# A hybrid recurrent trunk layer: the down projection's residual rows, affine steps, gated sums and buffers are rearranged

## The chip, the cores and the metric

The program runs on one core of a Trainium2 chip. The metric is the device time of one execution in microseconds. Engines are called as the profile calls them: PE (TensorE), DVE (VectorE), ACT (ScalarE), POOL (GpSimd) and SP, whose queue issues nearly all DMAs. Each engine works through its own queue in order.

## The reference, cut to what matters

2048 latent tokens and 128 context tokens pass one layer: a mixer with an input and an output projection, a norm, a SwiGLU feed-forward network (FFN) and a second norm. What the change touches is the part from the first norm on:

```python
    y, s_f, s_b = hybrid_mixer(h, ...)
    x = layer_norm(DEEPNORM_ALPHA * x + gate1 * y, ln1_g, ln1_b)
    h = x * (1.0 + scale2) + shift2
    ffn = (jax.nn.silu(h @ w_ffn_gate) * (h @ w_ffn_up)) @ w_ffn_down
    x = layer_norm(DEEPNORM_ALPHA * x + gate2 * ffn, ln2_g, ln2_b)
```

The model width is 1024, the FFN width 2816. All tensors are float32.

## The kernel before

**Arithmetic.** Tokens are handled in 17 rows of 128 tokens (16 of latents, one of context, number NS = 16). Each float32 factor of a matmul is split into a rounded high half (a copy on ACT, L129) and the low remainder (a subtraction, on DVE at L135, or on POOL at L133 if asked). `mm3` (L138 to L140) then issues three matmuls, high by high, high by low and low by high.

**Out projection** (lines from L1220 on). For each row it loads y and x (`xr`), multiplies out of PSUM by the gate (L1241), adds `ALPHA * x` (L1247), takes the norm's statistics (L893, L895; 1/std in two short POOL steps, L886 and L887), and normalises with one tensor_scalar (L1249). The normalised row, without the norm's gain and bias, is stored to `x1_d` (L1250); it is also transposed for the FFN, whose matrices take gain and bias in another place. `xr` has two buffers, in turns.

**Down projection** (from L1325). One level of a seven-product scheme (as in Strassen-Winograd) computes the product of activations and down weights: both are halved along the FFN width, the weights along the output columns, the tokens in pairs of rows. The combined activations lie in `dA[0..6]`, the combined weights in `td`. The stage has two halves `g` of eight rows each; a half has seven products `o`, a product eleven k-tiles, in six steps `kk` of two (the last of one), with four PSUM tiles (cells `q`). So one product has 11 x 4 x 3 = 132 matmuls of 512 columns. The leftover row (context) adds 33 matmuls to products 0, 2, 3 and 4 of the second half (`lk`), and to product 3 also a second weight (`wx`).

Every step loads raw weights (`ws`, three buffers, or `x0..`/`x2..`, kept from the first half for products 0 and 2) and raw activations (`as`, two buffers), and splits both (`wh`/`wl`, `ah`/`al`, three buffers each). After a product its four PSUM tiles are copied or added into cell tiles `c0`, `c1` (PSUM has seven buffers for them). A residual row is loaded from `x1_d`, and POOL multiplies it by the first norm's gain and adds its bias, both scaled by ALPHA (L1410, L1411). `fold` multiplies a finished sum by the gate (L1425), adds it to the row (L1426) and takes statistics (L1427). `finish` normalises the row on DVE (L1439) and applies the second norm's gain and bias on POOL (L1442, L1443), then stores it. The deferred steps stand in a list `bg`, from which one is taken after each step `kk` (BG = 1).

In the very last product the cells are computed one after the other from its third step on (KZ = 2), with split weights and activations in extra buffers; `last_fin` then ends the four last rows, two with ACT and POOL steps, two on DVE (L1450 to L1473).

**What sets the order.** A planner orders each engine's queue from the program order, from priorities (the first two steps of the stage are raised by DP = 400) and from a model of durations. Pools are stacked in SBUF; a tile at an address that a tile of an earlier stage held waits for that tile's last use.

## Time and profile before

| | us |
|---|---|
| median of 3 runs (2572.86 to 2576.82) | 2573.5 |
| profiled execution | 2574.1 |
| its span, first to last instruction | 2572.1 |

| engine | busy us | share of the span |
|---|---|---|
| PE | 2430.5 | 94% |
| DVE | 1953.7 | 76% |
| ACT | 1045.2 | 41% |
| POOL | 292.5 | 11% |

The profile is of one execution. A busy share is an average over stages; a stage is read from a window. In the lists a line such as `wl<-ws,wh` means an instruction that writes tile `wl` and reads `ws` and `wh`. A line number can be that of a helper (L129, L133, L135, L138 to L140), so tiles tell more than lines. "Idle before" is the time in which the engine stood still before an instruction, with what ended it.

### The profile page before, as it was taken

The numbers are of one execution on the slowest core, as the hardware profiler recorded it, in microseconds if no ns is written. First come the engines' busy times: TensorE is split into PE (matmuls) and PEld (weight loads), VectorE is DVE, ScalarE is ACT, GpSimd is POOL, SyncE is SP. The second block draws the span as 40 slices with busy tenths as digits, with TensorE's granted clock in tenths as the row PEclk, the third lists the DMA queues.
The fourth block names the chain that finished last, engine by engine and source line by source line (L and its number), as shares of the span: only waits on it lengthen the run. The fifth ranks groups of instructions, "written<-read, shape, count | busy, mean of one in ns | idle before, by whom it ended". The sixth has DMA issues, their size and how long they took to land. (4 is left out here: it accounts for less than half of the span.)

```text
span 2572.1 us, 38336 instructions
## 1 busy us (share of the span) xinstructions
PE 2430.5 (94%) x14628; PEld 2195.1 (85%) x14628; DVE 1953.7 (76%) x2995; ACT 1045.2 (41%) x1660; POOL 292.5 (11%) x227
## 2 busy tenths in 40 slices
PE   8999999999998998999999999999999889888995
PEld 6888888998887787899999999999999768666774
DVE  7755666887767655588887888878998676897768
ACT  4434445646457332433333333344444333233431
POOL 0000000000000113000000000000000251654035
PEclk9999999999999999999999999999999899899997
DMA  8954543434545377656434655336543745535552
GB/s 319 304 173 136 160 157 101 153 117 149 159 131 166 117 235 232 217 188 198 149 110 141 191 203 188 127 124 219 208 170 112 268 158 190 199 128 161 186 175 106
DMA packets 264295, 445.32 MB, mean 173 GB/s; under 512 B 32048, under 2 KB 174640, under 8 KB 264112
## 3 DMA queue, kind: packets, MB, share of 16 engines
q1 hardware_dynamic: 245488, 374.47, 44.8%
q10 hardware_dynamic: 18624, 68.42, 7.7%
q8 instruction: 114, 1.87, 0.3%
q14 instruction: 69, 0.57, 0.1%
HBM read 311.86 MB, written 130.94 MB: 172 GB/s over the span
## 5 line engine op out<-in xcount | busy, mean ns | idle before, releaser
L1018 PE MATMUL g<-xh,gwl 128*128 128x384 f32 (+1 forms) x1848 | 607.1, 329 | 8.5 <-DVE gwl L135 8.5
L1016 PE MATMUL g<-xh,gwh 128*128 128x384 f32 (+1 forms) x1848 | 608.5, 329 | 0.1
L1017 PE MATMUL g<-xl,gwh 128*128 128x384 f32 (+1 forms) x1848 | 606.5, 328 | 1.5 <-DVE xl L135 1.5
L1018 PEld LDWEIGHTS g<-xh,gwl 128*128 128x128 f32 x1848 | 348.1, 188 | 10.6 <-DVE gwl L135 10.5
L1017 PEld LDWEIGHTS g<-xl,gwh 128*128 128x128 f32 x1848 | 348.3, 188 | 2.9 <-DVE xl L135 1.8
L1016 PEld LDWEIGHTS g<-xh,gwh 128*128 128x128 f32 x1848 | 348.1, 188 | 1.7 <-issue 1.0
L139 PE MATMUL da<-wl,ah 128*128 128x512 f32 x588 | 241.3, 410 | 32.3 <-DVE wl L135 32.2
L138 PE MATMUL da<-wh,ah 128*128 128x512 f32 x588 | 239.5, 409 | 13.3 <-ACT wh L129 7.2
L140 PE MATMUL da<-wh,al 128*128 128x512 f32 x588 | 239.9, 408 | 6.3 <-DVE al L135 6.3
L129 ACT ACTIVATE ah<-as 128x1024 fp32r<-128x1024 f32 x81 | 80.3, 991 | 293.6 <-PE da L139 169.9
L129 ACT ACTIVATE gwh<-raw 128x1024 fp32r<-128x1024 f32 x124 | 131.1, 1057 | 164.4 <-PE g L1017 131.0
L135 DVE TENSOR_TENSOR al<-as,ah 128x1024 fp32r<-128x1024 f32 x81 | 122.3, 1514 | 85.1 <-ACT ah L129 85.0
L1038 ACT ACTIVATE v<-v 128x384 f32<-128x384 f32 (+1 forms) x132 | 66.9, 507 | 286.4 <-DVE v L1035 284.8
L139 PEld LDWEIGHTS da<-wl,ah 128*128 128x128 f32 x588 | 115.2, 196 | 65.5 <-DVE wl L135 37.8
L135 DVE TENSOR_TENSOR gwl<-raw,gwh 128x1024 fp32r<-128x1024 f32 x124 | 151.3, 1220 | 23.2 <-ACT gwh L129 22.8
L1035 DVE TENSOR_TENSOR v<-g,c 128x768 f32<-128x768 f32 (+1 forms) x132 | 120.1, 910 | 50.8 <-PE g L1018 50.6
L138 PEld LDWEIGHTS da<-wh,ah 128*128 128x128 f32 x588 | 114.7, 195 | 42.7 <-DVE c L1557 7.5
L140 PEld LDWEIGHTS da<-wh,al 128*128 128x128 f32 x588 | 115.2, 196 | 34.6 <-DVE al L135 7.1
L1410 POOL TENSOR_TENSOR ta<-ta,l1r 128x1024 f32<-128x1024 f32 x8 | 23.5, 2942 | 963.6 <-DMA ta<-x_d 963.6
L182 DVE SCALAR_TENSOR_TENSOR jk<-wm,cb 128x1026 bf16<-128x1026 f32 x96 | 117.6, 1225 | 20.2 <-DMA wm<-in_wmT_dram 19.1
L129 ACT ACTIVATE gwh<-sa 128x1024 fp32r<-128x1024 f32 x93 | 98.1, 1055 | 82.7 <-PE g L1017 65.1
L135 DVE TENSOR_TENSOR gwl<-sa,gwh 128x1024 fp32r<-128x1024 f32 x93 | 113.6, 1222 | 11.5 <-ACT gwh L129 10.7
(415 smaller groups left out, 5364.1 us busy)
## 6 DMA issues: line engine op xcount, KB each, us to landing
raw<-in_w_gu_dram ACTq DMA_DIRECT2D x60, 1024.0 KB, 5.0
as<-dA SPq DMA_DIRECT2D x70, 512.0 KB, 3.8
wm<-in_wmT_dram SPq DMA_DIRECT2D x48, 513.0 KB, 5.0
ws<-td SPq DMA_DIRECT2D x40, 512.0 KB, 4.4
dA<-a SPq DMA_DIRECT2D x106, 192.0 KB, 1.9
hlo<-h_d SPq DMA_DIRECT2D x48, 192.0 KB, 4.1
hhi<-h_d SPq DMA_DIRECT2D x48, 192.0 KB, 4.1
xr<-in_x_dram SPq DMA_DIRECT2D x17, 512.0 KB, 4.0
```

The lines of the kernel that those rows point to most:

```text
L129: c_ = A.activation(hi, src, AF.Copy)
L135: V.tensor_tensor(lo, src, f(hi), op=ALU.subtract)
L138: PE.matmul(out, w[0], m[0], start=start, stop=False)
L139: PE.matmul(out, w[0], m[1], start=False, stop=False)
L140: PE.matmul(out, w[1], m[0], start=False, stop=stop)
L182: return V.scalar_tensor_tensor(out=jk, in0=wt, scalar=1.0, in1=cbt[i], op0=ALU.mult, op1=ALU.mult, accum_out=mod[:, i, j:j + 1])
L1016: PE.matmul(ps_, wh_[:, i, c], xh_[kt], start=kt == 0, stop=False)
L1017: PE.matmul(ps_, wh_[:, i, c], xl_[kt], start=False, stop=False)
L1018: PE.matmul(ps_, wl_[:, i, c], xh_[kt], start=False, stop=kt == 3)
L1035: V.tensor_tensor(v, ps_, c1 if p in (4, 5) else c0, op=ALU.add)
L1038: A.activation(v[:, 0], v[:, 0], AF.Silu)
L1410: G.tensor_tensor(tt, tt, gbr[0], op=ALU.mult)
```

## The change

- *First norm's affine.* The out projection loads the gain and bias rows itself (into buffers of the FFN weights' pool), scales them by ALPHA, and DVE multiplies and adds them to each normalised row; the result goes into the buffer of `xr` (for the last two rows into the other) and that finished residual row is stored to `x1_d`. In the down projection the POOL steps and their row tiles fall away; rows are loaded directly, at the end of products 0 and 1.
- *Second norm's affine.* Two scalar_tensor_tensor steps on DVE, (x - mean) * gain and * 1/std + bias, take the place of one DVE and two POOL steps; so for all rows, the last four too.
- *Gated sums.* Products 4, 5 and 6 are multiplied by the gate straight out of PSUM and added to the row; the sums of product 3 are gated and added to both rows early. The sum c1 += c0 goes from POOL to DVE.
- *Leftover row.* Its matmuls go from the second half to the first.
- *Weights.* Products 0 and 2 load and split their weights in both halves. The split weights of product 6 are kept from the first half (in `x0..`, `x2..`); the last product loads only activations.
- *Deferred steps* are taken in even portions, so that the list is empty at the end of each product.
- *Layout.* Row tiles move to a pool of their own behind the weights' (`dwpt`); two PSUM tiles are allocated and skipped at the start; TM goes from 2 to 5, mean and 1/std tiles to 4.

```diff
+        res = []
+        for i, c in enumerate("hl"):
+            r = gw.tile([P, 2, 512], F32, tag=f"gw{c}", name=f"l1r{i}").rearrange("p a b -> p (a b)")
+            SY.dma_start(r, ln1r[i:i + 1, :].broadcast_to([P, D]))
+            V.tensor_scalar(r, r, ALPHA, None, op0=ALU.mult)
+            res.append(r)
...
                 V.tensor_scalar(tt, tt, mv[:, 0:1], rs, op0=ALU.subtract, op1=ALU.mult)
-                SY.dma_start(x1_d[r0:r0 + P, :], tt)
+                r_ = t_ if tt is xr else xr
+                V.tensor_tensor(r_, tt, res[0], op=ALU.mult)
+                V.tensor_tensor(r_, r_, res[1], op=ALU.add)
+                SY.dma_start(x1_d[r0:r0 + P, :], r_)
...
-        for t in ("ta", "tb"):
-            for q in range(4):
-                wp.tile([P, D], F32, tag=f"{t}{q}", name=f"res{t}{q}")
-        wp.tile([P, D], F32, tag="tl", name="restl")
         dwr = sx.enter_context(tc.tile_pool(name="dwr", bufs=3, reuse_waits=R))
         dwr.tile([P, 2, 512], F32, tag="ws", name="resws")
+        for c in "hl":
+            dwr.tile([P, 2, 512], F32, tag=f"w{c}", name=f"resw{c}")
+        wpt = sx.enter_context(tc.tile_pool(name="dwpt", bufs=1, reuse_waits=R))
...
+            def two(cs, q):
+                V.scalar_tensor_tensor(out=tt[:, cs], in0=tt[:, cs], scalar=h["mv"][:, 0:1], in1=lr[0][:, cs],
+                                       op0=ALU.subtract, op1=ALU.mult)
+
+            def three(cs, q):
+                V.scalar_tensor_tensor(out=tt[:, cs], in0=tt[:, cs], scalar=h["rs"], in1=lr[1][:, cs],
+                                       op0=ALU.mult, op1=ALU.add)
+                q.dma_start(yp[0][:, cs] if tk == NS else ys[0, tk * P:tk * P + P, cs], tt[:, cs])
...
-        def last_fin(q, tk, ps_, st, gate):
+        def last_fin(q, tk, ps_, st):
             z, tt = cells[0][q], tb[q]
             V.tensor_tensor(z, ps_, gate[:, lo_], op=ALU.mult)
-            V.tensor_tensor(tt[:, lo_], tt[:, lo_], z, op=ALU.add)
+            add(tt[:, lo_], z)
             V.bn_stats(st[:, 0], tt[:, lo_])
...
+            one, two, three = norm_parts(tk, tt, st, f"l{q}")
+            one()
+            for cs in (lo_, hi_):
+                two(cs, None)
+            for cs, e in ((lo_, A), (hi_, SY)):
+                three(cs, e)
...
+                if (g, o) == (0, 0):
+                    for q in range(2):
+                        acc.tile([P, 512], F32, tag="da", name=f"skip{q}")
...
-                lk = g == 1 and o in (0, 2, 3, 4)
+                lk = g == 0 and o in (0, 2, 3, 4)
...
+                    if final:
+                        ws = w6[kk]
+                    else:
+                        ws = wsplit(wsrc(g, o, kk), nm, (f"x0{kk}", f"x2{kk}") if o == 6 else None)
+                        if o == 6:
+                            w6[kk] = ws
+                    as_ = asplit(g, o, kk, ("wh", "wl") if final and kk > 2 else None)
...
-                    for _ in range(BG):
-                        if bg:
+                    if not final:
+                        for _ in range(-(-len(bg) // (len(KP) - kk))):
                             bg.pop(0)()
...
                     elif o == 3:
                         V.tensor_tensor(c0, ps_, c0, op=ALU.add)
-                        G.tensor_tensor(c1, c0, c1, op=ALU.add)
+
+                        def sums(c0=c0, c1=c1):
+                            add(c1, c0)
+                            gated(c1, gh)()
+
+                        fins += [sums, row(a_, hi_, c1), row(b_, hi_, c1), gated(c0, gl), row(b_, lo_, c0)]
                     elif o == 4:
...
+                        t = temp()
+                        V.tensor_tensor(t, ps_, gh, op=ALU.mult)
+                        fins.append(row(a_, hi_, t, sts[q, 0]))
+                        fins.append((prs[q][0], a_, sts[q, 0]))
                     elif o == 5:
...
+                        V.tensor_tensor(c1, ps_, gh, op=ALU.mult)
+                        V.tensor_tensor(c0, ps_, gl, op=ALU.mult)
+                        fins += [row(b_, hi_, c1, sts[q, 1]), row(b_, lo_, c0)]
```

## Rows read from the trace of the kernel before

**Rows 1.** From the page: busy time of each engine over the span, its share, and the number of instructions.
```profile
PE 2430.5 (94%) x14628; PEld 2195.1 (85%) x14628; DVE 1953.7 (76%) x2995; ACT 1045.2 (41%) x1660; POOL 292.5 (11%) x227
```

**Rows 2.** Windows by stage: the out projection; the gap before the down projection; the down projection; an undisturbed stretch of it; most of the gate/up stage. Columns: stretch, its length, busy time of PE, PEld, DVE, ACT and POOL (instructions), the granted clock, DMA share, GB/s.
```profile
890.00:1090.00 200.00, 192.49 (x907) 159.06 (x906) 117.26 (x162) 58.28 (x82) 35.28 (x50) 0.97 0.68 223
2011.60:2019.10 7.50, 0.28 (x3) 0.01 (x2) 4.53 (x6) 3.53 (x4) 0.00 (x0) 0.67 0.67 219
2019.10:2552.90 533.80, 485.65 (x1980) 383.79 (x1980) 414.93 (x376) 178.92 (x215) 212.02 (x101) 0.94 0.53 174
2100.00:2200.00 100.00, 100.00 (x430) 80.53 (x429) 62.55 (x68) 35.80 (x39) 11.41 (x7) 1.00 0.52 169
1110.00:1990.00 880.00, 871.40 (x5226) 867.21 (x5225) 738.88 (x935) 336.00 (x423) 0.00 (x0) 1.00 0.49 165
```

**Rows 3.** The same view in slices of 20 us of the down projection; left out are the other slices.
```profile
2020.00:2040.00 20.00, 17.82 (x66) 13.99 (x66) 11.63 (x9) 7.08 (x7) 3.22 (x2) 0.81 0.91 320
...
2080.00:2100.00 20.00, 14.47 (x54) 10.97 (x53) 19.81 (x10) 9.48 (x14) 13.95 (x6) 0.83 0.53 161
...
2220.00:2240.00 20.00, 10.47 (x26) 7.70 (x26) 14.85 (x16) 4.09 (x5) 16.36 (x8) 0.57 0.54 168
2240.00:2260.00 20.00, 14.32 (x57) 11.19 (x56) 20.00 (x9) 4.11 (x5) 17.21 (x6) 0.91 0.55 202
...
2300.00:2320.00 20.00, 15.10 (x59) 11.27 (x58) 19.17 (x12) 6.30 (x9) 17.90 (x10) 0.95 0.42 138
...
2500.00:2520.00 20.00, 9.51 (x35) 7.34 (x34) 17.38 (x14) 2.95 (x3) 18.06 (x12) 0.73 0.45 155
```

**Rows 4.** The view of tile `da` (the products' PSUM tiles), engine PE: what ended PE's idle time before these matmuls, in us, and how often.
```profile
  DVE wl L135: 32.2, 11
  ACT wh L129: 7.2, 1
  DVE al L135: 6.3, 2
  DVE c L1557: 6.1, 2
```

**Rows 5.** DVE's groups of instructions with shapes kept apart, 2096 to 2136 us. Columns: line, operation, tiles and shapes, count, busy us, mean ns of one, idle before and its releaser.
```profile
L135 DVE TENSOR_TENSOR al<-as,ah 128x1024 fp32r<-128x1024 f32 x7 | 8.5, 1221 | 10.1 <-ACT ah L129 10.1
...
L1425 DVE TENSOR_TENSOR tm<-tm,gb 128x512 f32<-128x512 f32 x2 | 1.3, 686 | 0.0
```

**Rows 6.** The same view, 2045 to 2094 us.
```profile
L135 DVE TENSOR_TENSOR al<-as,ah 128x1024 fp32r<-128x1024 f32 x6 | 20.3, 3394 | 3.3 <-ACT ah L129 3.3
```

**Rows 7.** Two lines' own views (least, median and greatest duration in ns, first and last start in us): a statistics step on DVE and a row step on POOL.
```profile
L1427 DVE BATCH_NORM_STATS2 st<-ta x16: 634/684/689, 2137.2 to 2502.2; 128x6 f32<-128x512 f32 x16
...
L1410 POOL TENSOR_TENSOR ta<-ta,l1r x8: 2392/2930/3401, 2036.7 to 2253.3; 128x1024 f32<-128x1024 f32 x8
```

**Rows 8.** DVE's groups from 2050 us to the end, all shapes of a group together (a product has five splits of 1024 columns and one of 512); the last row is the own view of the leftover row's splits, with least, median and greatest ns.
```profile
L135 DVE TENSOR_TENSOR al<-as,ah 128x1024 fp32r<-128x1024 f32 x75 | 113.3, 1515 | 81.3 <-ACT ah L129 81.3
...
L135 DVE TENSOR_TENSOR wl<-ws,wh 128x1024 fp32r<-128x1024 f32 (+1 forms) x56 | 95.3, 1704 | 1.0 <-ACT wh L129 0.6
...
L135 DVE TENSOR_TENSOR ll<-ls,lh 128x256 fp32r<-128x256 f32 (+1 forms) x24 | 23.7, 989 | 1.0 <-ACT lh L129 1.0
...
L1425 DVE TENSOR_TENSOR tm<-tm,gb 128x512 f32<-128x512 f32 x20 | 21.6, 1096 | 0.0
...
L135 DVE TENSOR_TENSOR ll<-ls,lh x24: 282/418/2630, 2081.3 to 2465.6; 128x256 fp32r<-128x256 f32 x20, 128x128 fp32r<-128x128 f32 x4
```

**Rows 9.** DVE's timeline, three instructions in a row. Columns: start, duration, engine, line, operation.
```profile
2534.73 1.20 DVE L135 TENSOR_TENSOR at<-as,at 128x1024 fp32r<-128x1024 f32 x1
2535.86 0.68 DVE L1425 TENSOR_TENSOR c<-c,gb 128x512 f32<-128x512 f32 x1
2536.46 0.68 DVE L1562 TENSOR_TENSOR c<-c,gb 128x512 f32<-128x512 f32 x1
```

**Rows 10.** Own views of two lines of the out projection (least, median, greatest ns), and, from the second, what ended DVE's idle time before it (us, times).
```profile
L1247 DVE SCALAR_TENSOR_TENSOR tt<-xr,tt x12: 1218/1225/1228, 903.2 to 1050.0; 128x1024 f32<-128x1024 f32 x12
...
L1249 DVE TENSOR_SCALAR tt<-tt,mv,rs x12: 811/814/816, 909.0 to 1054.8; 128x1024 f32<-128x1024 f32 x12
...
  POOL rs L887: 17.5, 16
```

**Rows 11.** ACT's timeline at the start of the down projection: the first split of activations and the first of weights, with the idle time before it.
```profile
2013.21 1.04 ACT L129 ACTIVATE ah<-as 128x1024 fp32r<-128x1024 f32 x1
...
2017.99 1.06 ACT L129 ACTIVATE wh<-x 128x1024 fp32r<-128x1024 f32 x1 [1.68 <-DVE as L1095]
```

**Rows 12.** DMA issues of the down projection (first row) and of the out projection: queue, count, size, median us from issue to landing.
```profile
ws<-td SPq DMA_DIRECT2D x40, 512.0 KB, 4.4
...
xr<-in_x_dram SPq DMA_DIRECT2D x13, 512.0 KB, 4.0
...
x_d<-tt SPq DMA_DIRECT2D x12, 512.0 KB, 3.5
```

**Rows 13.** DVE's timeline behind the last matmul (2552.9): the eviction of the last cell, and the last steps of the two last rows.
```profile
2556.54 0.68 DVE L1450 TENSOR_TENSOR c<-da,gb 128x512 f32<-128x512 f32 x1
...
2561.36 3.41 DVE L1467 SCALAR_TENSOR_TENSOR tb<-tb,rsl,l2r 128x512 f32<-128x512 f32 x2 [2.89 <-POOL rsl L887]
...
2567.53 1.42 DVE L1467 SCALAR_TENSOR_TENSOR tb<-tb,rsl,l2r 128x512 f32<-128x512 f32 x2 [0.46 <-POOL rsl L887]
```

More of the change, by code (lines that the diff above doesn't have):

```diff
@@ L1448, in last_fin, with norm_parts, one @@
[L1448 removed]
+        def norm_parts(tk, tt, st, nm):
+            h = {}
+            def one():
+                h["mv"] = rx.tile([P, 2], F32, tag="mv", name=f"mv{nm}", bufs=4)
+                V.bn_aggr(h["mv"], st)
+                h["rs"] = rstd(h["mv"][:, 1:2], rx, nm)
+            def two(cs, q):
[5 more added lines that the diff above has]
+                q.dma_start(yp[0][:, cs] if tk == NS else ys[0, tk * P:tk * P + P, cs], tt[:, cs])
+            return one, two, three
@@ L1449, in last_fin, with rest @@
+        def finish(tk, tt, st):
+            one, two, three = norm_parts(tk, tt, st, f"d{tk}")
+            def rest():
+                two(slice(0, D), None)
+                three(slice(0, D), SY)
+            bg.extend((one, rest))
+        def last_fin(q, tk, ps_, st):
             z, tt = cells[0][q], tb[q]
             V.tensor_tensor(z, ps_, gate[:, lo_], op=ALU.mult)
-            V.tensor_tensor(tt[:, lo_], tt[:, lo_], z, op=ALU.add)
+            add(tt[:, lo_], z)
             V.bn_stats(st[:, 0], tt[:, lo_])
-            mv = rx.tile([P, 2], F32, tag="mv", name=f"mvl{q}")
@@ new lines, in body, with row, go, gated @@
+                gl, gh = gate[:, lo_], gate[:, hi_]
+                def row(tt, cs, t, st=None):
+                    def go():
+                        add(tt[:, cs], t)
+                        if st is not None:
+                            V.bn_stats(st[:, cs.start // 512], tt[:, cs])
+                    return go
+                def gated(t, g_):
+                    def go():
+                        V.tensor_tensor(t, t, g_, op=ALU.mult)
+                    return go
+                fins = []
@@ L1572, in body @@
-                if g == 1 and o in (2, 4):
-                    cs = lo_ if o == 2 else hi_
-                    lt = rx.tile([P, 512], F32, tag="tm", name=f"tml{o}", bufs=TM)
-                    A.activation(lt, L["ps"], AF.Copy)
-                    later.append((fold(tl, cs, gb1[1], lt, None, sts["l"]), (NS, tl, sts["l"]) if o == 4 else None))
-                for fn, fin in later:
-                    bg.append(fn)
-                    if fin:
-                        finish(*fin)
+                        V.tensor_tensor(c1, ps_, gh, op=ALU.mult)
@@ L1583, in _layout @@
+                for fn in fins:
+                    if isinstance(fn, tuple):
+                        finish(*fn)
+                    else:
+                        bg.append(fn)
 def _layout(i):
```

136 lines of the change are left out of this document (38 added, 98 removed).

## The prediction, on record before the result

> **What bounds the kernel now.** I read the busy shares first. TensorE (PE) is busy 94% of the span, VectorE (DVE) 76%, GpSimd (POOL) 11% [rows 1]; so a gain has to come from stretches in which PE stands still, or from the ends of stages. The change touches two stages. The windows by stage give the out projection (890 to 1090 us) and the down projection (first matmul 2019.1, last one ended 2552.9), with the gap before it (from 2011.6) and the tail after it [rows 2].
>
> In the out projection PE is busy 192.5 of 200 us, DVE 117.3. In the undisturbed 100 us of the down projection PE issues 430 matmuls, one per 0.2326 us; the whole stage has 1980 of them, so 460.6 us of work that takes 533.8. The stage loses 73.2 us, the gap in front of it is 7.5 us, the tail 19.2 us. Nearly 100 us lie open around 461 us of work; that is the ceiling of any gain here.
>
> The windows of 20 us say where: PE falls to 14.5, 10.5, 14.3, 15.1 and 9.5 us in five slices, and in each of them POOL is busy 13.9 to 18.1 us and DVE 14.9 to 20 [rows 3]; in the 100 us with 11 us of POOL work PE is full [rows 2]. The PE view names the releaser: 32.2 us of idle time ended by DVE's low half of a weight, 6.3 by that of an activation, 6.1 by a sum on DVE, 7.2 by the first weight split of the stage [rows 4]. That is 51.8 us; the rest of the 73 is matmuls at the lower of the two clock levels after such a pause (granted clock 0.57 and 0.73 in two of the slices [rows 3]).
>
> Why DVE is late shows when its lines are grouped in two stretches. Without POOL a split subtraction of 1024 columns takes 1.22 us and a 512-column product 0.69; with POOL working on residual rows the same subtraction takes 3.39 [rows 5, 6], and one of 256 columns, 0.42 in the median, up to 2.63 [rows 8]. Statistics, which read one tensor, take 0.63 to 0.69 us wherever they run [rows 7]. So two-input DVE work and two-input POOL work stand in each other's way, and one POOL row step costs 2.4 to 3.4 us itself [rows 7]. In the gate/up stage, with no POOL work at all, DVE is busy 738.9 of 880 us (84%) and PE 871.4 [rows 2]: DVE at 84% starves PE by 1% if POOL is quiet.
>
> **The change, part by part.**
>
> *Gains on POOL, removed.* The first norm's affine (2 POOL steps for each of 17 rows), the second norm's affine (2 steps for each of 13 rows, and of the 2 last rows that took that path), the 8 sums c1 += c0 and 2 splits leave POOL. POOL's 212 us in the stage [rows 2] become the short 1/std steps. The four DVE groups with most of the stretch, at 1.13 us for the mean split (five of 1.22, one of 0.69, as a product has them), shrink by 56 x 0.57 = 32, 75 x 0.38 = 29, 24 x 0.57 = 14 and 20 x 0.41 = 8 us [rows 8]: at least 83 us of DVE time go.
>
> *The same work, added on DVE in the stage.* Back to back, DVE starts 512-column steps 0.60 us apart and 1024-column ones 1.14 apart [rows 9]. The reordered sums need 22 steps of 512 for each cell and half instead of 18 and 19: 4 x (4 + 3) = 28 x 0.60 = 16.8 us. 13 rows get two scalar_tensor_tensor steps (1.14 each by their start distance, 1.22 long [rows 10]) for one tensor_scalar (0.81 long): 19.9 us. Two last rows get four half steps on DVE: 8 x 0.71 = 5.7 [rows 13]. The kept weights save four subtractions, 4.6. Sum +38 us. DVE comes to 415 - 83 + 38 = 370 us in a stage of some 470, 79%, under the 84% of the gate/up stage.
>
> *Peaks.* One product has 132 x 0.2326 = 30.7 us of matmuls; with the leftover rows (now in the first half) 38.4. A product's splits cost 2 x 6.3 us. The fullest is product 5 of the first half, which also finishes five rows: 12.6 + 5 evictions 3.0 + 5 row steps with statistics 6.0 + 5 x 2.5 = 34.1 us, against 30.7. Three more stand at 29.4 to 29.7 (product 4 and 5 of the second half, and its product 0). A 1/std round trip through POOL costs DVE about 1.1 us when nothing is ready (17.5 us in 16 waits [rows 10]). Three buffers of split weights and activations cover about two steps of 5 us. Remaining loss of the stage: at least 1% as in gate/up, 4.6; at most 3.4 + 17 such waits (19), so 22. I take 12, nearer the gate/up row, which is the same mixture of splits and evictions with POOL quiet. Gain 73.2 - 12 = 61 us.
>
> *Layout.* Counted from the base that both have, the split weights began 73.7 KB up (x0 24.6, rows 36.9, raw weights 12.3), inside the pool of gated activations, which starts at 69.7 KB; hence ACT's first weight split waited for DVE's last activation sum and ran at 2017.99, when the activation split had run at 2013.21 [rows 11]. Now the split weights lie 36.9 to 61.4 KB up, over inputs of the FFN that PE has read by 2011.6 at the latest. The two skipped PSUM tiles move the first four accumulators off banks that are evicted last. The next release is then the activation pair, 2013.2 + 2 x 1.2 = 2015.6. PE starts about 3.8 us earlier: between 0 (another tile is late) and 5.
>
> *Weights.* Raw weights of products 0 and 2 are no longer kept, 12 more loads; the pair of product 6 is kept, 6 fewer loads, ACT splits and subtractions in the last product. Weight loads land in 4.4 us [rows 12], two or three buffers ahead. The fullest product (second half, product 0) moves 5.8 MB of operands, 2.1 of finished rows and 2.1 of new rows in 30.7 us, 325 GB/s, as much as the busiest slice moved (320, [rows 3]). The row loads now go out in a lump on SP's queue, and a weight load behind four of them is some 7 us late, inside two buffers. Cost taken: 0; bounds 0 and 10.
>
> *Tail.* After product 5 of the second half DVE has 8 evictions 4.8, rows 7.2, half of the activation splits 3.1, and 4 x 4.7 for the last rows: 34 us, PE 30.7. The last row's own chain is 4.7 plus one 1/std wait, so DVE ends about 5.7 us after PE, and 3.15 us follow for the last store (2568.95 to 2572.1). That is 9 us; with a little backlog 10 instead of 19.2. Today the last cell is evicted at 2556.54, 3.6 us after its last matmul, behind a step of the row before it, whose 1/std comes 2.9 us late from a busy POOL [rows 13]. Bounds: 9 and 19. Gain 9.2.
>
> *Out projection, added.* Two DVE steps per row (17 x 2.28 = 38.8 us), two scalings, two loads; DVE goes from 59% to 79% of that stage. The store leaves 2.3 us later and from xr's buffer, so the load of the row two further on waits for the landing: 1.2 + 1.3 + 0.2 + 1.1 + 0.8 + 2.3 + 3.5 + 4.0 = 14.4 us from the sum on [rows 10, 12], while two rows take PE 22 us. Behind the store stand y loads and the next x on SP. Only the first four rows, which come in a burst, and the combos on POOL at 960 to 1000 are tight. One third buffer of the gate weights is held until the last row. Lower bound 0 (PE hides it), upper bound 15 (a third of 41); I take 4, for it stays below the gate/up share.
>
> Sum: 2574.1 (profiled execution, span 2572.1) - 61 - 3.8 - 9.2 + 4 = 2504.1; the median of the runs shown is 0.6 lower. I forecast 2504 us.
>
> **Rivals.**
> 1. *DVE is the bound in the full products.* The waits for 1/std fall into four or five products and every pause brings the lower clock. For it: 34.1 against 30.7. Against it: the planner can put splits into the wait. Loss 22 and as much again at the lower clock for a good half of it: 35 instead of 12, so 2527.
> 2. *The out projection pays.* Row stores hold xr, DVE's sum waits for it in order, and the yhl split stands behind. 15 instead of 4: 2515.
> 3. *Loading is the bound* in the first products of each half, or the tail stays as it is (the rows finish no sooner because DVE now does all): +10 in the one place or +9 in the other, 2515 to 2525. The tail case is the one where the change doesn't do what it says.
> 4. *Slower: the DVE queue itself is the limit, not POOL.* If two-input steps stay long with POOL quiet (because of the loads, say), nothing shrinks and 38 us are added to DVE in the slices in which it already decides: 2573.5 + 38 - 9 + 4 = 2607. It decides from the point where the stretch that goes is under 38 us. Against it: 1.22 in a stretch with 0.52 DMA share.
> The Trainium skill, "Perfetto Trace Analysis", section "Optimizing Scalar/DVE Operations", says that where DVE is saturated, handing work to ScalarE or even GpSimd may pay, and adds that GpSimd shares a read port with DVE, so that it might not. Its first half is rival 4; rows 5 and 6 bear out the second.
> 5. *Clean.* Residue 5 us, out projection free, tail 9: 2492.
>
> **Numbers.** Forecast 0.50, rival 1 0.17, rival 2 0.09, rival 3 0.12, rival 4 0.05, rival 5 0.07. From the low end, the clean case less nothing, to rival 1 with the out projection's 11 on top, 2538: 2490 to 2538 leaves out rival 4 and the ends of the others. A measurement of this kernel can't tell less than 0.2% (5 us) from no change. Faster by more 0.93, within 0.02, slower 0.05.
>
> **What would show it.** In the down projection: split subtractions of 1024 at 1.22 us throughout, POOL under 30 us busy, matmuls of da waiting for DVE under 12 us in total. First da matmul about 2015.5 (plus what the out projection lost), without a second wait. PE's end to the end of the span about 10 us. The out projection as long as before within 10 us, with DVE at 79%. It is wrong if split subtractions stay over 2 us, if idle PE time moves to "DMA" or to 1/std releasers, or if the out projection grows by more than 15 us.

## The result, and the profile after

The changed kernel takes 2509.5 us (median of 4 runs, 2505.45 to 2512.38) beside 2575.2 us for the kernel before in the same comparison (2572.86 to 2578.02): ratio 0.9743, 95% interval 0.9723 to 0.9764. That is 2.6% faster. The forecast was 2504 us, 5.5 us lower; the time lies in the range. The profiled execution took 2511.98 us.

From the page of the changed kernel, the row that answers to [rows 1]:

```profile
PE 2416.3 (96%) x14628; PEld 2188.6 (87%) x14628; DVE 1910.0 (76%) x3072; ACT 1036.5 (41%) x1648; POOL 104.8 (4%) x149
```

DVE issues 77 instructions more and is busy 44 us less; POOL loses 188 us. The windows by stage answer to [rows 2] (columns as there): the out projection, the gap before the down projection, the down projection, the tail, and the same stretch of the gate/up stage.

```profile
890.00:1090.00 200.00, 189.38 (x871) 154.31 (x870) 149.32 (x186) 48.30 (x65) 34.21 (x48) 0.97 0.67 223
2025.40:2029.10 3.70, 0.33 (x4) 0.07 (x2) 2.30 (x3) 2.44 (x4) 0.00 (x0) 1.00 0.51 161
2029.10:2498.90 469.80, 465.60 (x1980) 373.84 (x1980) 337.78 (x425) 172.85 (x206) 34.27 (x31) 0.99 0.65 213
2498.90:2510.20 11.30, 0.01 (x1) 0.00 (x0) 7.15 (x12) 0.00 (x0) 2.76 (x4) 0.63 0.25 94
1110.00:1990.00 880.00, 867.98 (x5189) 863.39 (x5190) 738.65 (x933) 334.96 (x422) 0.00 (x0) 1.00 0.50 169
```

The down projection takes 469.8 us instead of 533.8, for the same 1980 matmuls; its loss over 0.2326 us a matmul falls from 73.2 to 9.3 us. The gap falls from 7.5 to 3.7, the tail from 19.2 to 11.3. Against that, fewer matmuls lie in the fixed stretches of the out projection (871 instead of 907) and of gate/up (5189 instead of 5226). Both stages also start later here, so the stretches alone don't say how much longer they are; the account below does.

An account of the two profiled executions, in which stages are told apart by the first and last matmul that writes a stage's tiles: down projection -64.0, gap -3.8, tail -7.9, out projection (6000th matmul to the first of gate/up) +5.0, gate/up +3.7, and +5.0 in front of the 6000th matmul, where both kernels issue the same work. The sum is -62.0, the profiled times differ by 62.1. The 6000th matmul came between 844.7 and 850.8 us in the fourteen profiles of this study, so the 5.0 is variation between executions.

What ends PE's idle time in tile `da` answers to [rows 4]:

```profile
its engine sat idle before it (us, times) until:
  DVE al L135: 4.0, 2
  ACT ah L129: 3.4, 1
  DVE wl L135: 0.2, 1
```

The 44.6 us of waits for weights, sums and activations on DVE have become 4.2. The DVE groups of the down projection with shapes kept apart (columns as in [rows 5]) show why:

```profile
L135 DVE TENSOR_TENSOR al<-as,ah 128x1024 fp32r<-128x1024 f32 x68 | 82.6, 1217 | 76.9 <-ACT ah L129 76.8
L135 DVE TENSOR_TENSOR wl<-ws,wh 128x1024 fp32r<-128x1024 f32 x60 | 73.0, 1216 | 15.8 <-ACT wh L129 15.8
```

Every subtraction of 1024 columns now runs at the undisturbed 1.22 us of [rows 5], and DVE spends its idle time waiting for ACT, not the other way round.

### The profile page after: what moved, and what is told of

Same layout as the page of the kernel before. It is cut to its first block, busy times and chain, and to the rows that moved or that the text cites. A ratio compares the mean times of both kernels' runs of the same rounds, so it can differ in the third digit from the quotient of the medians.

```text
span 2510.2 us, 38335 instructions
## 1 busy us (share of the span) xinstructions
PE 2416.3 (96%) x14628; PEld 2188.6 (87%) x14628; DVE 1910.0 (76%) x3072; ACT 1036.5 (41%) x1648; POOL 104.8 (4%) x149
## 4 chain that ended last, share of the span: by engine, by line
PE 73%; DVE 11%; DMA 8%; ACT 4%; issue 2%; POOL 1%; SPq 1%; ACTq 0%; DVEq 0%; POOLq 0%
PE g L1018 10%; PE g L1017 10%; PE g L1016 10%; PE da L140 6%; PE da L139 5%; PE da L138 5%; PE ua L299 2%; PE asq L138 1%; PE asq L139 1%; PE oa L140 1%; PE asq L140 1%; PE oa L139 1%; PE azk L138 1%; PE oa L138 1%; PE azk L139 1%
## 5 line engine op out<-in xcount | busy, mean ns | idle before, releaser
L138 PE MATMUL da<-wh,ah 128*128 128x512 f32 x528 | 209.1, 397 | 3.4 <-ACT ah L129 3.4
L140 PE MATMUL da<-wh,al 128*128 128x512 f32 x528 | 209.5, 397 | 0.6 <-DVE al L135 0.6
L139 PE MATMUL da<-wl,ah 128*128 128x512 f32 x528 | 209.6, 397 | 0.2 <-DVE wl L135 0.2
L135 DVE TENSOR_TENSOR al<-as,ah 128x1024 fp32r<-128x1024 f32 x81 | 91.6, 1132 | 89.6 <-ACT ah L129 89.4
L138 PEld LDWEIGHTS da<-wh,ah 128*128 128x128 f32 x528 | 99.5, 188 | 27.6 <-ACT ah L129 3.6
L140 PEld LDWEIGHTS da<-wh,al 128*128 128x128 f32 x528 | 99.6, 189 | 25.1 <-DVE al L135 0.9
L139 PEld LDWEIGHTS da<-wl,ah 128*128 128x128 f32 x528 | 99.6, 189 | 24.9 <-DVE wl L135 0.7
L135 DVE TENSOR_TENSOR wl<-ws,wh 128x1024 fp32r<-128x1024 f32 x72 | 81.2, 1128 | 16.0 <-ACT wh L129 15.8
```

The costliest lines, as they stand in the source:

```text
L135: V.tensor_tensor(lo, src, f(hi), op=ALU.subtract)
L138: PE.matmul(out, w[0], m[0], start=start, stop=False)
L139: PE.matmul(out, w[0], m[1], start=False, stop=False)
L140: PE.matmul(out, w[1], m[0], start=False, stop=stop)
```

## The experiments

Twelve kernels ran, in three groups, each beside its own runs of the kernel before. Times are medians; "against the changed kernel" compares with 2509.5 us. Stage lengths are those of the account above. The kernel before took 2573.1, 2575.6 and 2573.3 us in the three groups (2575.2 beside the changed kernel), so two or three microseconds between kernels of different groups are not told from noise.

**The two affines, one at a time, on the kernel before.** `e1_second_affine` takes only the second norm's affine from POOL to DVE (for the four last rows too), `e2_first_affine` only the first norm's, into the out projection. PQ and NOWV choose the path of the four last rows; with 0 and 4 all of them are finished on DVE.

```diff
-                V.tensor_scalar(tt, tt, mv[:, 0:1], rs, op0=ALU.subtract, op1=ALU.mult)
+                h[:] = [mv, rs]
 
             def two():
-                G.tensor_tensor(tt, tt, lr[0], op=ALU.mult)
-                G.tensor_tensor(tt, tt, lr[1], op=ALU.add)
+                mv, rs = h
+                V.scalar_tensor_tensor(out=tt, in0=tt, scalar=mv[:, 0:1], in1=lr[0], op0=ALU.subtract, op1=ALU.mult)
+                V.scalar_tensor_tensor(out=tt, in0=tt, scalar=rs, in1=lr[1], op0=ALU.mult, op1=ALU.add)
...
-PQ = 2
-NOWV = 2
+PQ = 0
+NOWV = 4
```

> The kernel before with only the second norm's affine moved from GpSimd to DVE (two scalar_tensor_tensor steps for every row, the last four too); first affine, sums, weights and layout as before. Theory (two-input work on GpSimd stretches two-input work on DVE, and late DVE starves TensorE): of the 64 row steps on GpSimd 30 go; the pauses at 2500 to 2520 and at 2300 to 2320 and about half of those at 2220 to 2260 shrink, the tail falls from 19 to about 12 us: 2548 us, 2535 to 2560. Rival (DVE's amount of work is the limit, GpSimd is a bystander): DVE gets 26 us more in the slices in which it decides: 2585 to 2600.

```diff
-                SY.dma_start(x1_d[r0:r0 + P, :], tt)
+                r_ = t_ if tt is xr else xr
+                V.tensor_tensor(r_, tt, res[0], op=ALU.mult)
+                V.tensor_tensor(r_, r_, res[1], op=ALU.add)
+                SY.dma_start(x1_d[r0:r0 + P, :], r_)
...
-                G.tensor_tensor(tt, tt, gbr[0], op=ALU.mult)
-                G.tensor_tensor(tt, tt, gbr[1], op=ALU.add)
```

> The kernel before with only the first norm's affine moved into the out projection on DVE. Theory (port): the pauses at 2020 to 2100 and at 2320 to 2350 and part of those at 2220 to 2260 go, some 35 us; the out projection pays 5 to 7: about 2546 us, 2535 to 2560. The two single moves together give less than or about as much as the whole change (66 us) if the affine steps are the whole of it. Rival (layout, kept weights and reordered sums carry the gain): e1 and e2 together give under 25 us. Rival (amount of DVE work): here DVE loses no work of its own in the down projection, so no gain there and 5 to 7 us lost: 2580.

Measured: 2536.6 us for the first (ratio 0.9858, 0.9844 to 0.9873), 2560.0 for the second (0.9948, 0.9932 to 0.9965): -36.6 and -13.2, together -49.8 of the 65.6 us. The second's down projection became 25.2 us shorter (508.6), but its out projection and gate/up grew by 4.7 and 4.4. POOL's work of the stage falls to 143.7 and 112.8 us, and the mean subtraction of an activation with it, from 1654 ns to 1608 and 1327:

```profile
L135 DVE TENSOR_TENSOR al<-as,ah 128x1024 fp32r<-128x1024 f32 x66 | 105.8, 1608 | 66.6 <-ACT ah L129 66.5
```

```profile
L135 DVE TENSOR_TENSOR al<-as,ah 128x1024 fp32r<-128x1024 f32 x66 | 87.3, 1327 | 104.1 <-ACT ah L129 104.1
```

(the first row is of `e1_second_affine`, the second of `e2_first_affine`, both over the down projection). So a part of the stretch goes with each part of the POOL work, and neither affine alone gets all of it. The down projections of the two, in this order:

```profile
2022.20:2515.30 493.10, 473.01 (x1980) 375.58 (x1980) 387.43 (x380) 177.39 (x213) 143.67 (x70) 0.99 0.58 189
2030.80:2539.40 508.60, 477.93 (x1980) 379.64 (x1980) 346.46 (x374) 178.31 (x215) 112.82 (x67) 0.96 0.55 181
```

The stage is 40.7 and 25.2 us shorter, together 65.9, about as much as the whole change gives there (64.0). What the two lack of the 65.6 us of time lies at the ends of the stage: their gaps are 8.0 and 8.7 us and their tails 20.5 and 19.3, as long as before or longer. `e2_first_affine` has less POOL work and shorter subtractions than `e1_second_affine`, and still loses more (48.0 against 32.5 us), so the mean stretch alone doesn't give the loss. Rival 4 had DVE's own queue as the limit: it wanted the time to rise when work goes from POOL to DVE, and here it falls in both runs.

**Is it POOL's reading, or POOL being busy?** Both kernels are the changed one with scratch work added on POOL behind each finished row's statistics (13 rows): four products of 1024 columns that read two tensors, or eight fills of 1024 columns that read none. Nothing of the layer is left out.

```diff
             def rest():
+                G.tensor_scalar(zz[:, 0:1], st[:, 0, 0:1], 0.0, None, op0=ALU.mult)
+                for _ in range(4):
+                    G.tensor_tensor(zz, zz, lr[0], op=ALU.mult)   # e3
+                for _ in range(8):
+                    G.memset(zz, 0.0)                             # e4
```

> The changed kernel with idle work added: behind the statistics of each of the 13 finished rows GpSimd multiplies a scratch tile of 1024 columns by a gain row four times (two tensors read, nobody waits for the result), 52 steps, some 125 us of GpSimd. Theory (port): split subtractions beside them take 2.5 to 3.4 us again, TensorE waits for DVE again in the products that finish rows, 15 to 35 us in all: 2525 to 2545. Rival (GpSimd's work never mattered by itself, only the chain row, affine, store did): no change, 2505 to 2513.

> The same with eight memsets of the scratch tile in the place of the four products: GpSimd is busy at the same places but reads nothing. Theory (it is the reading of SBUF by GpSimd that two-input DVE steps collide with): split subtractions stay at 1.22 us and the time at 2505 to 2513. Rival (any GpSimd work, its writes or its instruction stream, holds DVE up): like the run with the products, 2520 or more.

Measured: 2590.6 us with the reads (ratio 1.0067, 1.0052 to 1.0082: the whole gain is gone and more), 2510.7 with the fills (0.9762, 0.9748 to 0.9777: no change). POOL's scratch steps in its groups over the down projection (columns as for DVE), with reads:

```profile
L1443 POOL TENSOR_TENSOR zz<-zz,l2r 128x1024 f32<-128x1024 f32 x52 | 152.6, 2934 | 3.9
```

and with fills:

```profile
L1443 POOL MEMSET zz<- 128x1024 f32 x104 | 99.4, 956 | 5.6
```

The window of the stage with reads, and under it with fills:

```profile
2021.60:2574.90 553.30, 488.94 (x1980) 386.32 (x1980) 432.12 (x425) 173.16 (x206) 194.49 (x96) 0.93 0.55 181
```

```profile
2025.60:2496.80 471.20, 466.88 (x1980) 374.97 (x1980) 337.87 (x425) 172.78 (x206) 156.14 (x148) 0.99 0.65 213
```

POOL is busy 194 and 156 us (in the second, 18.2 us of it are the record of one single small step), but DVE's time for the same 425 instructions is 432 and 338 us: 94 us more beside reads, nothing beside fills. DVE's groups beside the reads:

```profile
L135 DVE TENSOR_TENSOR al<-as,ah 128x1024 fp32r<-128x1024 f32 x68 | 99.5, 1465 | 62.7 <-ACT ah L129 62.4
L135 DVE TENSOR_TENSOR wl<-ws,wh 128x1024 fp32r<-128x1024 f32 x60 | 91.9, 1531 | 17.2 <-ACT wh L129 16.9
...
L135 DVE TENSOR_TENSOR wl<-ws,wh 128x512 fp32r<-128x512 f32 x12 | 14.7, 1224 | 0.1
L1543 DVE TENSOR_TENSOR tm<-tm,gb 128x512 f32<-128x512 f32 x8 | 14.3, 1782 | 0.0
...
L1537 DVE BATCH_NORM_STATS2 st<-ta 128x6 f32<-128x512 f32 x16 | 10.8, 683 | 0.0
```

Steps that read two tensors of SBUF stretch, the statistics, which read one, do not. DVE also waits for 1/std behind the products, 12.7 us in all against 1.7 in the changed kernel; behind the fills it waits 6.4 us and the time is unchanged, so this is at most a small part of the 81 us. The waits of PE in `da` are as long as in [rows 4] or a little longer: 36.7 us for `wl` and 9.4 for `al`.

```profile
  DVE wl L135: 36.7, 11
  DVE al L135: 9.4, 5
```

The Trainium skill, "SBUF — State Buffer", section "Who interferes with whom", says that a DVE instruction with two SBUF inputs contends with a GpSimd instruction that reads SBUF, not with one that only writes it. These two runs agree with both halves of it: +94 us of DVE time beside reads, none beside fills. No run has POOL read a single tensor.

**The layout.** `e5_old_place` puts the split weights of the changed kernel back to where they lay before; `e9_no_skip` takes out the two skipped PSUM tiles.

```diff
+        dws = sx.enter_context(tc.tile_pool(name="dws", bufs=3, reuse_waits=R))
+        dws.tile([P, 2, 512], F32, tag="ws", name="resws")
+        wpt = sx.enter_context(tc.tile_pool(name="dwpt", bufs=1, reuse_waits=R))
+        for t in ("ta", "tb"):
+            for q in range(4):
+                wpt.tile([P, D], F32, tag=f"{t}{q}", name=f"res{t}{q}")
+        wpt.tile([P, D], F32, tag="tl", name="restl")
         dwr = sx.enter_context(tc.tile_pool(name="dwr", bufs=3, reuse_waits=R))
-        dwr.tile([P, 2, 512], F32, tag="ws", name="resws")
         for c in "hl":
             dwr.tile([P, 2, 512], F32, tag=f"w{c}", name=f"resw{c}")
-        wpt = sx.enter_context(tc.tile_pool(name="dwpt", bufs=1, reuse_waits=R))
...
```

> The changed kernel with the split weights of the down projection back at their old place (row tiles in front of them, 73.7 KB up, over the gated activations); the raw weights and everything else as changed, the two skipped PSUM tiles too. Theory (the address of the split weights made the pause before the stage): the pause between the last FFN matmul and the first one of the stage goes from 3.7 to about 8 us, the first weight split waits for DVE's last activation sum again, total 4 to 6 us more, about 2515. Rival (the skipped PSUM tiles, or the earlier raw loads, made it short): the pause stays at 3.7.

```diff
-                if (g, o) == (0, 0):
-                    for q in range(2):
-                        acc.tile([P, 512], F32, tag="da", name=f"skip{q}")
```

> The changed kernel without the two skipped PSUM tiles. If the rest of the layout (split weights below the gated activations) is what shortened the gap, the gap before the down projection stays at 3.7 us and the time at 2509 +- 3. If the skipped tiles carry part of it, the first accumulators wait for the last evictions of the gate/up stage: gap 5 to 7.5 us, time 2511 to 2514.

Measured: 2520.9 us with the old place (0.979, 0.9773 to 0.9808), 11.4 more than the changed kernel, with a gap of 12.0 us; 2508.8 without the skipped tiles (0.9748, 0.9729 to 0.9766), gap 3.7, no change. ACT's timeline at the gap with the old place, columns as in [rows 11]:

```profile
2028.07 1.06 ACT L129 ACTIVATE ah<-as 128x1024 fp32r<-128x1024 f32 x1 [4.37 <-DMA as<-dA]
2029.03 0.40 ACT L129 ACTIVATE lh<-ls 128x256 fp32r<-128x256 f32 x1
2031.59 1.06 ACT L129 ACTIVATE wh<-ws 128x1024 fp32r<-128x1024 f32 x1 [2.17 <-DVE as L1095]
```

and in the changed kernel:

```profile
2026.66 0.47 ACT L1038 ACTIVATE v<-v 128x320 f32<-128x320 f32 x1 [3.05 <-DVE v L1035]
2027.04 1.04 ACT L129 ACTIVATE wh<-ws 128x1024 fp32r<-128x1024 f32 x1
2027.99 1.04 ACT L129 ACTIVATE ah<-as 128x1024 fp32r<-128x1024 f32 x1
```

At the old place the first weight split waits for the activation sum on DVE, as in [rows 11]. DVE's timeline there:

```profile
2029.15 1.23 DVE L135 TENSOR_TENSOR al<-as,ah 128x1024 fp32r<-128x1024 f32 x1 [4.17 <-ACT ah L129]
...
2031.09 0.42 DVE L1095 TENSOR_TENSOR as<-a,a 128x256 f32<-128x256 f32 x1
```

The sum (L1095) stands in DVE's queue behind the second subtraction of activations, and that one waits for ACT, whose split waited 4.37 us for its load; in the kernel before the same split waited 1.01 us. So the wait is longer than before; why that load lands later here, no run shows. At the new place the split follows directly on the last FFN activation. The skipped tiles carry nothing.

**The down projection's other parts.** `e6_reload` loads and splits product 6's weights in the second half again, `e7_left_late` gives the leftover row back to the second half.

```diff
-                    if final:
-                        ws = w6[kk]
-                    else:
-                        ws = wsplit(wsrc(g, o, kk), nm, (f"x0{kk}", f"x2{kk}") if o == 6 else None)
-                        if o == 6:
-                            w6[kk] = ws
+                    ws = wsplit(wsrc(g, o, kk), nm, (f"x0{kk}", f"x2{kk}") if o == 6 else None)
```

> The changed kernel with the weights of product 6 loaded and split again in the second half (no kept pair). Theory A (less split work in the last product is a good part of the shorter tail): DVE gets 6.3 us more in and just before the last product, where it has 34 us of work beside 30.7 us of matmuls; the tail goes from 11.3 to 15 to 17 us, total 2514. Theory B (what I predicted: the tail shrinks because no row waits for GpSimd): tail 11 to 12, total unchanged within 2 us.

```diff
-                lk = g == 0 and o in (0, 2, 3, 4)
+                lk = g == 1 and o in (0, 2, 3, 4)
```

> The changed kernel with the leftover row's matmuls and its finishing back in the second half. Theory A (it crowds DVE in the last products): the row's sum, norm and store fall beside product 5 of the second half, tail 12 to 14, total 2 to 4 us more. Theory B (order of halves is indifferent): same within 2 us, and the products 3 to 5 of the first half lose less.

Measured: 2508.5 us (0.9738, 0.9723 to 0.9753) and 2504.8 (0.9724, 0.971 to 0.9739). Keeping the weights is worth nothing that can be measured. With the leftover row late, the stage's loss is 4.3 us instead of 9.3, and the wait for `al` in tile `da` falls from 4.0 to 0.6 us. The window of its down projection, and that wait:

```profile
2027.70:2492.50 464.80, 463.90 (x1980) 372.92 (x1980) 336.93 (x423) 172.91 (x206) 34.50 (x30) 1.00 0.65 214
```

```profile
  DVE al L135: 0.6, 1
```

The pause that goes is one of 3.3 us, ended at 2253.2 by the first subtraction of activations of the first half's product 6. It follows on product 5, which finishes five rows when the leftover row is there.

**The tail.** `e12_old_sums` gives the second half its old order of gated sums.

```diff
                     elif o == 5:
-                        V.tensor_tensor(c1, ps_, gh, op=ALU.mult)
-                        V.tensor_tensor(c0, ps_, gl, op=ALU.mult)
-                        fins += [row(b_, hi_, c1, sts[q, 1]), row(b_, lo_, c0)]
+                        V.tensor_tensor(c1, ps_, c1, op=ALU.add)
+                        V.tensor_tensor(c0, ps_, c0, op=ALU.add)
+                        fins += [gated(c1, gh), row(b_, hi_, c1, sts[q, 1]), gated(c0, gl), row(b_, lo_, c0)]
```

(for the second half alone; products 3 and 4 likewise)

> The changed kernel with the gated sums of the second half in the order of before (products 3 to 5 summed out of PSUM, gated and added to the rows afterwards: 8 steps of 512 columns, 4.8 us, more behind product 5). If that order is what kept VectorE busy behind the last matmul in the run with the second norm's affine alone (tail 20.5 us): the tail grows from 11.3 to 15 to 20 us, time 2513 to 2518. If the short tail comes from the last four rows' own steps: tail 11 to 13, time 2509 to 2512.

Measured: 2513.0 us (0.9768, 0.9751 to 0.9785), tail 14.0 us instead of 11.3. That lies under the 15 to 20 that the theory wanted, so the order of sums is a part of it only. More is seen in `e1_second_affine`, where all four last rows are on DVE and the tail is nevertheless 20.5 us. DVE's timeline there, from the last product on; its matmuls ended at 2515.3:

```profile
2492.21 2.31 DVE L1445 SCALAR_TENSOR_TENSOR ta<-ta,mvd,l2r 128x1024 f32<-128x1024 f32 x1
...
2500.97 1.27 DVE L1446 SCALAR_TENSOR_TENSOR tl<-tl,rsd,l2r 128x1024 f32<-128x1024 f32 x1
...
2512.98 0.68 DVE L1427 BATCH_NORM_STATS2 st<-tb 128x6 f32<-128x512 f32 x1
2513.58 1.27 DVE L1453 TENSOR_TENSOR c<-da,gb 128x512 f32<-128x512 f32 x2
...
2524.40 0.67 DVE L1453 TENSOR_TENSOR c<-da,gb 128x512 f32<-128x512 f32 x1
```

DVE still finishes rows of earlier products until 2502 and gated sums until 2513; the first cell of the last product is evicted at 2513.58, the last at 2524.40, 9.1 us after its matmuls. In the changed kernel:

```profile
2484.54 0.69 DVE L1446 TENSOR_TENSOR c<-da,gb 128x512 f32<-128x512 f32 x1 [0.23 <-PE da L140]
...
2500.08 1.41 DVE L1429 SCALAR_TENSOR_TENSOR tb<-tb,rsl,l2r 128x512 f32<-128x512 f32 x2 [0.45 <-POOL rsl L887]
2501.41 0.68 DVE L1446 TENSOR_TENSOR c<-da,gb 128x512 f32<-128x512 f32 x1
...
2505.70 1.41 DVE L1429 SCALAR_TENSOR_TENSOR tb<-tb,rsl,l2r 128x512 f32<-128x512 f32 x2 [0.46 <-POOL rsl L887]
```

there the first cell is taken as soon as PE has it, and the last 2.5 us after its matmuls end at 2498.9.

**The out projection.** `e8_affine_down` keeps the changed kernel's first affine on DVE but does it in the down projection, two steps for each loaded row (TM goes from 5 to 3 to make room); `e10_both` is that with the leftover row of `e7_left_late`; `e11_gate_row` adds to that a gate of the context row spread with one matmul for four.

```diff
-                V.tensor_tensor(r_, tt, res[0], op=ALU.mult)
-                V.tensor_tensor(r_, r_, res[1], op=ALU.add)
-                SY.dma_start(x1_d[r0:r0 + P, :], r_)
+                SY.dma_start(x1_d[r0:r0 + P, :], tt)
...
+            def two():
+                V.tensor_tensor(tt, tt, res[0], op=ALU.mult)
+                V.tensor_tensor(tt, tt, res[1], op=ALU.add)
+
+            bg.append(two)
```

> The changed kernel with the first norm's affine on DVE in the down projection, where rows are loaded, and not in the out projection (TM is 3 to make room). Theory (DVE has room in the stage as long as GpSimd is quiet): out projection back to its time of before (5 us less), the first FFN steps too (2 to 4 less), DVE in the stage 338 + 39 = 377 of 470 us, stage loss 9 to 15: total 2503, 2498 to 2510. Rival (DVE is at its limit in the full products): stage loss 25 to 40, total 2520 to 2535.

> The two edits that each beat the changed kernel, together: the leftover row's matmuls in the second half again, and the first norm's affine on VectorE in the down projection. If their gains are independent (one lies in product 5 of the first half, the other in the out projection): 2509 - 5 - 10 = 2494 to 2496. If the affine's steps and the leftover row's now meet in the first products of the second half: 2499 to 2502, the stage's loss 10 to 15 us.

```diff
-                gate_row(gb0[1], gbp, lambda nm: acc.tile([P, 512], F32, tag="acc", name=nm), 1, 16, "01")
+                for hh in range(2):
...
+                    dg = op.tile([P, 4, P], F32, tag="dg", name=f"dg01{hh}", bufs=1)
+                    for j in range(4):
...
+                        V.tensor_scalar(dg[:, j], ident, mod[:, 1, c_:c_ + 1], None, op0=ALU.mult)
+                    PE.matmul(ps_, ones, dg.rearrange("p a b -> p (a b)"), start=True, stop=True)
```

> As e10_both, and in the out projection the context row's gate is spread over the partitions with four VectorE products into one tile and one matmul of 512 columns, twice, in place of eight products and eight matmuls that wait for one another through one buffer. If the waits of that spot (2.4 + 1.5 + 5.8 us between 972 and 988 in the changed kernel) are those of the one buffer: 5 to 8 us less than e10_both, about 2488. If they hide a wait for a row's statistics that comes next anyway: within 2 us of e10_both.

Measured: 2499.9 us (0.9703, 0.9688 to 0.9717), 2497.3 (0.9702, 0.9683 to 0.9721) and 2499.8 (0.9716, 0.9697 to 0.9735). In the first the out projection is 228.0 us instead of 234.0 and gate/up 935.1 instead of 940.5, as long as in the kernel before; the down projection takes up the affine for 1.3 us. Its windows of the out projection and the down projection:

```profile
890.00:1090.00 200.00, 191.07 (x910) 157.61 (x909) 116.03 (x163) 58.45 (x83) 34.32 (x50) 0.99 0.68 225
2012.90:2484.00 471.10, 466.88 (x1980) 374.79 (x1980) 376.24 (x461) 173.25 (x206) 34.97 (x31) 0.99 0.65 215
```

So DVE at 376 of 471 us (80%) costs PE nearly nothing in a stage with POOL quiet, and 33 us more of DVE work in the out projection (149.3 instead of 116.0) cost 11.4 us with what follows, 6.0 in the stage itself and 5.4 in gate/up. The longest wait that grew is that of the gate row. What PE waited for in tile `gbp`, first in the changed kernel, then in `e8_affine_down`:

```profile
  DVE dg L148: 8.1, 3
```

```profile
  DVE dg L148: 4.3, 3
```

But the waits for the transposes (tile `tp`) are shorter in the changed kernel, 2.2 us against 4.4 in `e8_affine_down`. All waits of PE between the 6000th matmul and gate/up come to 15.1 us in the changed kernel, 13.0 in `e8_affine_down` and 12.1 in the kernel before. The other 3.9 of the 6.0 us are PE's own time: it is busy 218.7 us with this work at a granted clock of 0.96, against 214.8 at 0.99 in `e8_affine_down`.

The second edit adds nothing that can be told from `e8_affine_down`: the pause behind product 5 goes, but one of 1.9 us for an activation split comes, ended at 2053.2, at the start of product 1, where the affines of the first rows now stand. In the third, PE's wait for `dg` shrinks to 2.0 us, but the next wait grows with it, that of the transposes for ACT's copies of earlier ones, from 2.9 us in `e10_both` to

```profile
  ACT ho L1173: 6.7, 1
```

so the gate row's waits hid one behind them, the second of the two expectations. No run made this edit with the affine in the out projection. `e8_affine_down` and `e10_both` beat both kernels, by 10 to 12 us over the changed one.

## Why the prediction was right, and where it was off

**The down projection, 61 us forecast, 64.0 measured: right.** The mechanism is the one that the prediction named, and it is shown from both sides: POOL's work taken away shortens DVE's steps, reading put back on POOL lengthens them again (+81 us), filling does not. Taken one at a time, the two affines shorten the stage by 65.9 us in sum, the whole change by 64.0. All splits run at 1.22 us, PE's waits for DVE are 4.2 us (under 12 was wanted). POOL's busy time is 34.3 us, a little over the 30 named; its short 1/std steps take that. Two sizes were off, both to the good side. DVE's time came to 338 us, not 370. With the 38 us of added work this means that some 115 us of stretch went, not 83; the four groups of [rows 8] left out smaller ones. And the loss left is 9.3 us, not 12.

**The fullest product: right in its place, not in its reason.** Product 5 of the first half was said to overfill DVE (34.1 against 30.7 us). The only pause of any size behind the stage's start, 3.3 us, follows on it, and that goes when the leftover row does (`e7_left_late`). But DVE was not late with product 5: it waited 1.03 us for PE before that product's first eviction at 2245.91. What PE waited for is product 6's first subtraction of activations, which stands behind eight evictions and the leftover row's last step and starts at 2251.90; in `e7_left_late` it starts at 2209.71, ahead of the evictions that begin at 2213.24. In the second half of that run product 5 finishes the same five rows (there the next product's weights are kept), and no pause follows. By the timelines the order in DVE's queue made this pause, and not the sum of its work; no run changed the order alone. Rival 1 let such waits fall into four or five products; there is one.

**The layout, 3.8 forecast, 3.8 measured: right in size, and in cause for one of its two parts.** The address of the split weights is the cause, and with the other parts in place it is worth more than the difference of the gaps, 8.3 us of gap in `e5_old_place`. The two skipped PSUM tiles, which the prediction also counted, do nothing.

**The kept weights, 0 forecast: right** (`e6_reload`, within 1 us).

**The tail, 9.2 forecast, 7.9 measured: right in size, wrong in its reason.** The step that failed is "behind a step of the row before it, whose 1/std comes 2.9 us late from a busy POOL". [rows 13] has them the other way round: the last cell is evicted at 2556.54, and the step that waited 2.89 us starts at 2561.36, behind it. That wait and the long step after it (3.41 us, where the last row's takes 1.42) are gone from the tail after, but they did not hold up the eviction. And with that POOL work gone (`e1_second_affine`, where DVE has the steps of two more last rows instead) the tail is 20.5 us. What holds up the cells there is DVE's backlog: gated sums and finished rows of earlier products stand in front of them. The kernel before had a backlog too; its first two cells were evicted together, with no idle time of DVE before them:

```profile
2545.47 1.27 DVE L1450 TENSOR_TENSOR c<-da,gb 128x512 f32<-128x512 f32 x2
```

The old order of sums gives back 2.7 us of the 9.2 between 20.5 and 11.3, the weights' reload 0.9, the leftover row 0.7. The finished rows that are left over, which the change takes in even portions before each product's end, are the likely rest, some 5 us; e1's timeline shows them in the last product, but no run changed that alone, so it is argued and not shown. The last row's own chain came out as forecast, 5.7 us from the eviction of its cell (2501.41) to DVE's end; the eviction itself comes 2.5 us behind the last matmul.

**The out projection, +4 forecast, 9 to 11 measured: the term that was mis-sized.** Its bounds, 0 to 15, held it; the value was taken near the lower end because DVE's share would stay below that of gate/up. DVE came to 75% of the stretch, under that share as forecast, and yet the edit cost 5.0 us there and 3.7 in gate/up by the two profiles (6.0 and 5.4 by `e8_affine_down`). The cost is no chance of one execution: in the nine profiles with the affine in the out projection this stage takes 232.4 to 234.9 us and gate/up 937.5 to 941.7, in the five without it 228.0 to 230.4 and 934.9 to 937.0. So an average share did not decide. PE's waits grew in two places. One is at the gate row of the context, where eight short products on DVE and eight matmuls take turns through one buffer; but the waits for the transposes shrank, and of the 6.0 us against `e8_affine_down` only 2.1 are waits. The other is gate/up, where PE waits 13.6 us in all, against 9.9 in `e8_affine_down` and 10.0 in the kernel before. A part of that lies at its start: what ended PE's waits in tile `g` before 1250 us was, in the changed kernel and in `e8_affine_down`:

```profile
  DVE gwl L135: 4.8, 5
  DVE xl L135: 3.1, 2
```

```profile
  DVE gwl L135: 3.5, 3
  DVE xl L135: 1.5, 1
```

No run changed one of these waits with the affine in place, so where the 9 to 11 us arise is read from the profiles and not shown. Rival 2 priced this stage at 15 and so lies as far off on the other side.

The sum 2504.1 missed the median by 5.4 us. By the account above this term is 4.7 of that and the tail 1.3, and the down projection gave 3.0 back; the other 2.4 lie within the variation between executions. Rival 4, the slower one, is excluded by `e1_second_affine` and `e2_first_affine`, where the same move makes the kernel faster; rival 3's tail that stays did not come, nor did a bound by loads (the DMA share of the stage rose from 0.53 to 0.65 without a wait for one in `da`).

## What to carry to other kernels

Work on POOL that reads two tensors of SBUF is not free beside a DVE that works on two-tensor steps: look at one and the same DVE instruction in a stretch with POOL and in one without, and count the difference as the price of the POOL work; here 64 us of the down projection hung on it, and 81 us when it was put back, though both engines looked far from full. When the work then goes to DVE, the busy share of a stage doesn't say what it will cost: the same affine cost 1.3 us at 80% of the down projection and 9 to 11 at 75% of the out projection and behind it. Try it in each stage that can hold it. A tail behind the last matmul is best read from the first eviction of the last product: if the engine was not ready for it, there is a backlog in front, and the last rows' own steps are not the whole cause.

## What the runs showed of the hardware that was not expected

The size of the contention. Of `e3_pool_reads` 15 to 35 us were expected; 52 POOL products, 152.6 us of POOL time off the critical path, cost 81 us at the end, half a microsecond for each of POOL's. Both sides pay: the POOL products themselves take from 2.34 to 3.46 us each, by what DVE does beside them, and a DVE subtraction of 512 columns (`wl`) goes from 0.68 to 1.22 in the mean. And the other half of it: 99.4 us of POOL fills in the same places left DVE's subtractions at 1.217 us and the time of the kernel where it was.

It is not two-tensor steps alone that stretch. In the kernel before, the normalising step L1439 reads one tensor of SBUF and two columns of scalars, and it took up to 2.82 us instead of 0.81 (least, median and greatest ns, as in [rows 10]):

```profile
L1439 DVE TENSOR_SCALAR ta<-ta,mvd,rsd x8: 799/812/2821, 2197.2 to 2508.4; 128x1024 f32<-128x1024 f32 x8
```

The long one, at 2229.33, starts 0.1 us behind a POOL row step of 2.35 us. The statistics (0.68 us) and the sums that DVE takes out of PSUM with one tensor of SBUF (`c<-da,c`, 0.68) kept their time beside POOL's products in `e3_pool_reads`.
